# An unused 32-byte tile ahead of the weight buffers in SBUF: a conv and MLP block in fp32 on one core

## The chip, the cores and the metric

The kernel runs on one core of one Trainium2 chip. The metric is device time in microseconds (us) of one execution. Three executions of the kernel before took 1090.11, 1090.36 and 1090.12 us; the median is 1090.12 us.

## What is computed

One decoder layer on 256 tokens of width 2048, all in float32: a modulation from the condition vector c, a gated causal depthwise convolution, and an MLP of width 8192 with squared ReLU.

```python
cond = silu(c)
sh1, sc1, g1, sh2, sc2, g2 = split(cond @ mod_w + mod_b, 6)
h = rms_norm(x, norm1_g) * (1 + sc1) + sh1
a, gt = split(h @ conv_w_in + b_in, 2)          # 2048 -> 2 x 2048
u = depthwise_conv(a * sigmoid(gt), 31 taps) + dw_b
y = silu(layer_norm(u, ln_g, ln_b)) @ conv_w_out + b_out
x = x + (1 + g1) * y
h = rms_norm(x, norm2_g) * (1 + sc2) + sh2
u = square(relu(h @ mlp_w1))                    # 2048 -> 8192
x = x + (1 + g2) * (u @ mlp_w2)                 # 8192 -> 2048
```

## The kernel before, in words

**How the work is staged.** A list of jobs runs in this order: 16 jobs "in" (two 128-column blocks of conv_w_in each; the first 8 are computed together during the start), 8 jobs "out", then four quarters of the MLP with 8 jobs "up" (mlp_w1) and 8 jobs "down" (mlp_w2) each. Between them matrix-vector work for the modulation and the convolution is woven in. The order of the instructions on each engine comes from a planner that simulates a timeline, with orders put by hand where `issue_after` stands; the loads are issued by SP in the order of the list `order` (L541 to L550), each as soon as a buffer of its kind is free (`top_up`, L175).

**How a product of two float32 matrices is made.** A weight block of 1 MB comes by DMA into one of seven buffers `raw` (L181, 128 partitions of 8192 bytes). ScalarE writes the rounded part into tiles `hi` (L216), VectorE or GpSimd the rest into `lo` (L220), in halves of 4096 bytes per partition; both have the type fp32r. Activations are split in the same way into `hl` (what enters the jobs in, out and most of up) or `u2` (what enters the jobs down and, as `xa`, the first two of up). Three products hi x hi, lo x hi and hi x lo are then summed in PSUM.

In the jobs "in" and the first two "up" the weights are the stationary operand, in "out" too, in a form with 256 columns:

```python
nc.tensor.matmul(p[:, c, :], hi[:, k % HALF, :], m, ...)                       # L245, 512 columns
nc.tensor.matmul(p[:, c, T : 2 * T], lo[:, k % HALF, :], m[:, 0:T], ...)       # L246, 256 columns
nc.tensor.matmul(out_p, w, m[:, 0:T], start=begin, stop=False)                 # L241, L242, L243: 256 columns
```

In the other jobs up and down the activations are stationary, and the split weights move, 512 columns at a time (L282 to L284):

```python
hi, lo = [w[:, 4 * (k % 2) : 4 * (k % 2) + 4, :]... for w in parts[...]]
p_hi, p_lo = [m[:, n : n + P] for n in (t * P, T + t * P)]
nc.tensor.matmul(p, p_hi, hi, ...); nc.tensor.matmul(p, p_hi, lo, ...); nc.tensor.matmul(p, p_lo, hi, ...)
```

Products in plain float32 (not split) are the held first product of the jobs in (L609, weights `first`, activations `two`), the modulation rows (L336), the convolution on TensorE (L826) and column sums with the tile `ones` (L454). In the trace each of these stands as two instructions.

**Where the tiles lie.** Pools are stacked in SBUF in the order in which they are opened, and a tile starts at a multiple of 32 bytes. From the left come const, wts, acts, tmp, early and then, one after the other, start, conv or res; from the right come the pool of the four `cv` tiles with `mu` and later `pad` (L1052, 752 floats that nothing reads or writes) with `u2`. From the sizes of the tiles follow these first bytes in a partition (sizes in brackets):

| tile | first byte | past a multiple of 64 | past a multiple of 256 | past a multiple of 4096 |
|---|---|---|---|---|
| v (4624), ones (512), cz (2240) | 384, 14144, 14656 | 0 | 128, 64, 64 | 384, 1856, 2368 |
| warm (8), the last of const | 17408 | 0 | 0 | 1024 |
| raw, 7 x 8192 | 17440 | 32 | 32 | 1056 |
| hi, 6 x 4096; lo, 6 x 4096 | 74784; 99360 | 32 | 32 | 1056 |
| hl, 8 x 4096 | 123936 | 32 | 32 | 1056 |
| two, 6 x 2048 | 157728 | 32 | 32 | 2080 |
| u2, 8 x 4096 (from the right) | 193568 | 32 | 32 | 1056 |

All blocks of one kind are a multiple of 2048 bytes apart, and every operand of L241 to L246 and L282 to L284 starts a multiple of 512 bytes into its tile. The tap sums of the convolution on VectorE and ScalarE (L705, L738) read `u` from byte 4 x j of a tile on, for tap j; the matmuls L826 start 16 bytes further from one step m to the next.

Of the kernel before, what the change touches and what calls it, by code (L numbers as in the profile page):

```python
# [8 lines left out]
F32 = mybir.dt.float32  # L9
# [5 lines left out]
P = 128  # L15
# [58 lines left out]
def conv_block(ctx: ExitStack, tc: tile.TileContext, x, vec, dwq, c_row, mod_r, mod_t, mod_c, w_first, w_in, w_out, w1, w2, out):  # L74
    nc = tc.nc

    const = ctx.enter_context(tc.tile_pool(name="const", bufs=1))
# [50 lines left out]
        nc.vector.tensor_scalar(col("modb", w * KT, KT), col("modb", w * KT, KT), 1.0, None, op0=ALU.add)  # L128
    amps = {w: const.tile([P, KT], F32, name=f"amp{w}") for w in (SC1, SC2)}
    warm = const.tile([P, 2], F32, name="warm")  # L130
    other = warm[:, 1:2]

    def table(func, after):
# [1087 lines left out]
```

## Time and profile before

| what | value |
|---|---|
| median of the runs | 1090.12 us |
| span of the profiled execution, first to last instruction | 1088.4 us |
| the rest, between the span and the median | 1.7 us |
| instructions in the profile | 15427 |
| matmuls, weight loads | 6000, 6000 |

The profile was taken from one execution; its own whole time is not listed, so its span stands beside the median of the three runs. Line numbers are those of the kernel. PE is TensorE, PEld its weight loads, DVE is VectorE, ACT is ScalarE, POOL is GpSimd, SP is the engine that issues the DMAs. A matmul's duration in the trace includes the time in which it overlaps the next one, so the pace of TensorE is read from the distance between starts.

### The profile page before, as it was taken

To read this page: it belongs to the slowest core of one execution; us is meant where nothing else is said; L and a number is where in the kernel's file an instruction comes from. 1 tells how busy PE (TensorE), PEld (TensorE's weight loads), DVE (VectorE), ACT (ScalarE), POOL (GpSimd) and SP (SyncE) were. 2 spreads that over 40 slices of the span, in tenths; PEclk is the share of its full clock that TensorE was granted. 3 is DMA by queue.
4 is the path that set the end of the run, shared out by engine and by line. 5 is a ranking of instruction groups with operands and counts; after the bars stand their busy time and mean duration, and the time that the engine had idled before them with its cause. 6 is when DMAs were issued, how large, how long until landed. Compare 5 with 4: busy or idle time off the path is not lost.

```text
span 1088.4 us, 15427 instructions
## 1 busy us (share of the span) xinstructions
PE 1072.4 (99%) x6000; PEld 890.4 (82%) x6000; DVE 750.0 (69%) x1022; ACT 520.3 (48%) x707; POOL 214.6 (20%) x147
## 2 busy tenths in 40 slices
PE   6999999999999999999999999999999999999998
PEld 3888876777799988888888888888888888888887
DVE  5777799989668877778845676545565665565653
ACT  4111398776876585444444444333444333444431
POOL 0000069989498260000000000000000000000000
PEclk8999999999999999999999999999999999999999
DMA  9999997997999967999967899667888776788611
GB/s 383 420 420 421 415 418 296 375 362 272 406 409 399 363 244 237 276 288 384 390 237 227 237 283 329 202 152 291 242 237 245 222 217 212 232 251 239 212 64 39
DMA packets 142315, 314.21 MB, mean 289 GB/s; under 512 B 87585, under 2 KB 105505, under 8 KB 107297
## 3 DMA queue, kind: packets, MB, share of 16 engines
q1 hardware_dynamic: 142096, 313.10, 82.0%
q8 instruction: 47, 0.77, 0.3%
q14 instruction: 26, 0.21, 0.1%
q10 hardware_dynamic: 146, 0.13, 0.0%
HBM read 301.13 MB, written 12.07 MB: 288 GB/s over the span
## 4 chain that ended last, share of the span: by engine, by line
PE 88%; DMA 8%; DVE 2%; ACT 1%; issue 0%; ACTq 0%; SPq 0%; DVEq 0%
PE mm L283 20%; PE mm L282 20%; PE mm L284 20%; DMA raw<-mod_c 7%; PE mm L245 6%; PE mm L246 3%; PE acc L242 2%; PE acc L241 2%; PE acc L243 2%; PE mm L826 2%; PE row L336 2%; DVE raw L428 1%; PE mm L609 1%; DMA v<-vec 1%; PE mm L241 0%; PE mm L242 0%
## 5 line engine op out<-in xcount | busy, mean ns | idle before, releaser
L216 ACT ACTIVATE hi<-raw 128x1024 fp32r<-128x1024 f32 x320 | 335.3, 1058 | 358.2 <-PE mm L284 330.3
L220 DVE TENSOR_TENSOR lo<-raw,hi 128x1024 fp32r<-128x1024 f32 x259 | 314.5, 1220 | 184.0 <-ACT hi L216 182.2
L283 PE MATMUL mm<-lo,u 128*128 128x512 f32 x496 | 193.0, 389 | 0.0
L282 PE MATMUL mm<-hi,u 128*128 128x512 f32 x496 | 193.0, 389 | 0.0
L284 PE MATMUL mm<-hi,u 128*128 128x512 f32 x496 | 192.9, 389 | 0.0
L284 PE MATMUL mm<-hi,hl 128*128 128x512 f32 x480 | 186.7, 389 | 0.0
L283 PE MATMUL mm<-lo,hl 128*128 128x512 f32 x480 | 186.7, 389 | 0.0
L282 PE MATMUL mm<-hi,hl 128*128 128x512 f32 x480 | 186.7, 389 | 0.0
L220 POOL TENSOR_TENSOR lo<-raw,hi 128x1024 fp32r<-128x1024 f32 x61 | 153.5, 2546 | 31.9 <-ACT hi L216 31.9
L428 DVE SCALAR_TENSOR_TENSOR raw<-raw,cond 128x2048 f32<-128x2048 f32 x50 | 116.5, 2332 | 39.3 <-DMA raw<-mod_c 39.3
L284 PEld LDWEIGHTS mm<-hi,u 128*128 128x128 f32 x496 | 93.1, 188 | 19.3
L283 PEld LDWEIGHTS mm<-lo,u 128*128 128x128 f32 x496 | 93.1, 188 | 19.1
L282 PEld LDWEIGHTS mm<-hi,u 128*128 128x128 f32 x496 | 93.1, 188 | 19.0
L284 PEld LDWEIGHTS mm<-hi,hl 128*128 128x128 f32 x480 | 90.1, 188 | 18.7
L282 PEld LDWEIGHTS mm<-hi,hl 128*128 128x128 f32 x480 | 90.1, 188 | 18.7
L283 PEld LDWEIGHTS mm<-lo,hl 128*128 128x128 f32 x480 | 90.1, 188 | 18.7
L705 DVE SCALAR_TENSOR_TENSOR acc<-u,v,acc 128x256 f32<-128x256 f32 x230 | 91.5, 480 | 0.0
L245 PE MATMUL mm<-hl,hi 128*128 128x512 f32 x224 | 80.0, 401 | 0.0
L609 PE MATMUL mm<-two,first 128*128 128x256 f32 x240 | 57.0, 392 | 8.2 <-ACT two L667 8.0
L241 PE MATMUL acc<-hl,hi 128*128 128x256 f32 x224 | 63.4, 283 | 0.0
L242 PE MATMUL acc<-hl,hi 128*128 128x256 f32 x224 | 63.4, 283 | 0.0
L243 PE MATMUL acc<-hl,lo 128*128 128x256 f32 x224 | 63.4, 283 | 0.0
(223 smaller groups left out, 1286.7 us busy)
## 6 DMA issues: line engine op xcount, KB each, us to landing
raw<-w SPq DMA_DIRECT2D x128, 1024.0 KB, 5.5
raw<-mod_c SPq DMA_DIRECT2D x64, 1024.0 KB, 11.2
raw<-mod_r SPq DMA_DIRECT2D x28, 1024.0 KB, 9.2
raw<-w_in SPq DMA_DIRECT2D x16, 1024.0 KB, 10.9
raw<-w_out SPq DMA_DIRECT2D x16, 1024.0 KB, 7.7
first<-w_first SPq DMA_DIRECT2D x15, 1024.0 KB, 19.8
flat<-two SPq DMA_DIRECT2D x30, 256.0 KB, 2.7
two<-flat SPq DMA_DIRECT2D x120, 64.0 KB, 4.2
```

The lines of the kernel that those rows point to most:

```text
L216: state["w_hi"] = nc.scalar.activation(hi, w[:, ks, :], AF.Copy).ins
L220: end = by.tensor_tensor(lo, w[:, ks, :], hi.bitcast(F32), op=ALU.subtract)
L241: nc.tensor.matmul(out_p, w, m[:, 0:T], start=begin, stop=False)
L242: nc.tensor.matmul(out_p, w, m[:, T : 2 * T], start=False, stop=False)
L243: state["mm_end"] = nc.tensor.matmul(out_p, lo[:, k % HALF, :], m[:, 0:T], start=False, stop=end)
L245: nc.tensor.matmul(p[:, c, :], hi[:, k % HALF, :], m, start=(k == 0), stop=(k == KT - 1))
L282: nc.tensor.matmul(p, p_hi, hi, start=begin, stop=False)
L283: nc.tensor.matmul(p, p_hi, lo, start=False, stop=False)
L284: nc.tensor.matmul(p, p_lo, hi, start=False, stop=end)
L428: end = nc.vector.scalar_tensor_tensor(w, w, 1.0, cb, op0=ALU.mult, op1=ALU.mult, accum_out=acc)
L609: step = nc.tensor.matmul(held[n][:, c, :], w[:, 2 * n + c, :], h, start=k == 0 and c == 0, stop=k == KT - 1, skip_group_check=True)
L705: end = nc.vector.scalar_tensor_tensor(out, s, w, acc, op0=ALU.mult, op1=ALU.add)
```

## The change

One more tile is allocated in the pool const, after `warm` and ahead of everything in the pools that follow. Nothing writes or reads it. It has 8 floats, so 32 bytes in each partition.

```diff
     amps = {w: const.tile([P, KT], F32, name=f"amp{w}") for w in (SC1, SC2)}
     warm = const.tile([P, 2], F32, name="warm")
+    const.tile([P, 8], F32, name="shift_all")
     other = warm[:, 1:2]
```

So raw, hi, lo, hl, two and all that is stacked on them from the left begin 32 bytes further: raw at 17472, hi at 74816, hl at 123968, each 1088 bytes past a multiple of 4096 and 0 past a multiple of 64. The tiles of const itself, the cv tiles, mu and u2 stay where they are.

## Rows read from the trace of the kernel before

**Rows 1.** The page: its first line and part 1.

```profile
span 1088.4 us, 15427 instructions
PE 1072.4 (99%) x6000; PEld 890.4 (82%) x6000; DVE 750.0 (69%) x1022; ACT 520.3 (48%) x707; POOL 214.6 (20%) x147
```

**Rows 2.** Busy time by stretch: PE, PEld, DVE, ACT, POOL, clock, DMA share, GB/s.

```profile
30.00:117.00 87.00, 84.28 (x387) 72.92 (x386) 62.42 (x85) 13.57 (x26) 0.00 (x0) 1.00 1.01 420
390.00:1085.00 695.00, 694.56 (x3167) 577.76 (x3159) 436.41 (x465) 299.35 (x321) 13.96 (x6) 1.00 0.76 240
```

**Rows 3.** The chain that ended last: its shares by line, and one piece.

```profile
by line: PE mm L283 20.3%; PE mm L282 20.3%; PE mm L284 20.3%; DMA raw<-mod_c 7.3%; PE mm L245 6.3%; PE mm L246 3.1%; PE acc L241 2.5%; PE acc L242 2.5%; PE acc L243 2.5%; PE mm L826 2.0%; PE row L336 1.8%; DVE raw L428 1.4%; PE mm L609 0.9
...
54.87 19.86 DMA raw<-mod_c
```

**Rows 4.** Instructions in time, PE, job down: start us, duration us.

```profile
479.86 0.39 PE L282 MATMUL mm<-hi,u 128*128 128x512 f32 x1
...
493.46 0.39 PE L282 MATMUL mm<-hi,u 128*128 128x512 f32 x1
```

**Rows 5.** The same view, PE, job up.

```profile
575.74 0.39 PE L282 MATMUL mm<-hi,hl 128*128 128x512 f32 x1
...
589.34 0.39 PE L282 MATMUL mm<-hi,hl 128*128 128x512 f32 x1
```

**Rows 6.** The same view, PE, jobs out: 256 columns.

```profile
321.02 0.28 PE L241 MATMUL acc<-hl,hi 128*128 128x256 f32 x1
...
332.90 0.28 PE L241 MATMUL acc<-hl,hi 128*128 128x256 f32 x1
```

**Rows 7.** The chain, pieces of plain float32 matmuls: start, length, count.

```profile
127.45 1.73 PE acc L609 x8
...
162.17 3.59 PE mm L826 x64
165.76 3.43 PE row L336 x32
...
199.21 0.86 PE small L454 x4
```

**Rows 8.** Groups of instructions by line: busy us, mean ns.

```profile
L705 DVE SCALAR_TENSOR_TENSOR acc<-u,v,acc 128x256 f32<-128x256 f32 x230 | 91.5, 480 | 0.0
L738 ACT ACTIVATE cv<-u,v 128x256 f32<-128x256 f32 x22 | 9.3, 497 | 0.0
...
L1080 ACT ACTIVATE two<-x,amp 128x256 f32<-128x256 f32 x16 | 7.2, 496 | 0.0
...
L844 DVE SCALAR_TENSOR_TENSOR u<-mm,v,two 128x256 f32<-128x256 f32 x12 | 5.7, 482 | 3.3 <-ACT two L842 3.2
```

**Rows 9.** Instructions in time, PE: pairs L245 and L246, job in, then job up.

```profile
152.12 0.40 PE L245 MATMUL mm<-hl,hi 128*128 128x512 f32 x1
...
153.18 0.40 PE L245 MATMUL mm<-hl,hi 128*128 128x512 f32 x1
...
402.86 0.39 PE L245 MATMUL mm<-u,hi 128*128 128x512 f32 x1
...
408.75 0.39 PE L245 MATMUL mm<-u,hi 128*128 128x512 f32 x1
```

**Rows 10.** Matmuls that read u2 (first), then hl: ns min/median/max, first and last start.

```profile
L282 PE MATMUL mm<-hi,u x496: 389/389/396, 474.4 to 1078.0; 128*128 128x512 f32 x166
...
L282 PE MATMUL mm<-hi,hl x480: 387/389/391, 409.1 to 996.0; 128*128 128x512 f32 x160
...
L245 PE MATMUL mm<-hl,hi x224: 393/398/504, 136.5 to 250.7; 128*128 128x512 f32 x112
...
L241 PE MATMUL acc<-hl,hi x224: 283/283/283, 297.8 to 380.4; 128*128 128x256 f32 x112
```

**Rows 11.** Last use of the tiles part; the split that writes the seventh u2.

```profile
L740 POOL TENSOR_TENSOR cv<-cv,part x8: 731/741/749, 178.1 to 228.9; 128x256 f32<-128x256 f32 x8
...
361.27 0.63 ACT L228 ACTIVATE u<-two 128x512 fp32r<-128x512 f32 x1
```

## The prediction

> **What bounds the kernel now.** I read the page first. TensorE is busy for 1072.4 of 1088.4 us and VectorE, the next, for 750.0 [rows 1], so what moves an address on VectorE, ScalarE or GpSimd matters only where TensorE waits for it. Then the busy time by stretch. From 30 to 117 us the DMA share stands at 1.01 with 420 GB/s: this start is bound by loads. From 390 us to the end TensorE is busy for 694.56 of 695.00 us, while DMA is at 0.76 [rows 2]. The chain of waits says the same: L282 to L284 hold three times 20.3%, L245 and L246 9.4%, L241 to L243 7.5%, and the only transfers of weight are those into raw from mod_c, 7.3%, in pieces like the one of 19.86 us [rows 3]. So the time is about 80 us of loads and 950 us of matmuls one behind the other, and the question is whether a matmul, or a load, goes faster or slower from an address 32 bytes on.
>
> A matmul's own duration includes overlap, so I take distances between starts. In a job down, 60 steps (20 rounds of L282, L283, L284) lie between the two starts shown: (493.46 - 479.86) / 60 = 226.7 ns [rows 4]. In a job up the same 60 steps take (589.34 - 575.74) / 60 = 226.7 ns [rows 5]. With 256 columns, 99 steps take (332.90 - 321.02) / 99 = 120.0 ns [rows 6]. The difference, 106.7 ns for 256 columns, is 0.417 ns a column; 512 columns are then 213.4 ns, and 13.3 ns of every fp32r matmul do not depend on its length. Plain float32 does otherwise: eight of L609 take 1.73 us, so 216 ns for 256 columns, and 32 of L336, which run four at a time, take 3.43 us, so 429 ns for 512 [rows 7]. That is 213 ns for 256 columns, and about 3 ns fixed.
>
> **The change part by part.** *The tile itself.* It has no instruction: 0 us, and the planner has nothing new to order, so I expect the same instructions in the same order on each engine. That the tile takes room although unused follows from `pad`, which nothing uses either and which does push u2. The shift makes one new overlap between tiles from the left and from the right: the first buffer `part` ended at byte 201760, where a buffer u2 begins, and now ends 32 bytes inside it. If that adds a wait, it is for an addition that starts at 228.9 us at the latest, by a split at 361.27 us [rows 11]: 0 us.
>
> *VectorE, ScalarE, GpSimd.* The trace holds the experiment already. The tap sums L705 start at byte 4j of a tile, so at all offsets in a 64-byte block, and take 480 ns, as L844 with its fixed starts takes 482; on ScalarE the taps L738 take 497 ns and L1080, with fixed starts, 496 [rows 8]. 0 us, and what is left over would hide behind TensorE, which waits for none of them from 390 us on. GpSimd has no such pair of rows here; its 214.6 us [rows 1] lie beside the stretch that TensorE fills too. If that cover failed, a tenth of it would be 21 us, the far end of the slow side.
>
> *Plain float32 matmuls.* In L826 the moving operand starts 16 bytes further at each step m and the weights alternate between 0 and 32 past 64; its 64 instructions, four at a time, take 3.59 us, 224 ns a group with the last one's end in it. L454 reads its weights from `ones`, at 0 past 64, four in 0.86 us or 215 ns, where L609 with both operands at 32 takes 216 [rows 7]. 0 us.
>
> *Loads.* They land 32 bytes further, at 0 instead of 32 past a multiple of 64. No row here shows a full-rate load at both offsets. The stretch of 87 us moved 420 GB/s with no idle time [rows 2]; I bound this term by one 32-byte piece of the 8192 bytes of a partition, either way: 87 x 32 / 8192 = 0.34 us. I take 0 and keep -0.3 and +0.3. The Trainium skill, DMA: Bandwidth & Descriptors, section How a descriptor splits into AXI transactions, speaks against the change: a descriptor that starts off a multiple of 256 bytes also pays for the bytes below its start, so 8192 bytes from 32 past are 257 pieces of 32 bytes and from 64 past 258. By that rule the sum would be an estimated 0.3 us more, 1090.5; no run here shows it.
>
> *fp32r matmuls.* This is the term that decides, and the trace of before can't settle it: hi, lo, hl and u2 all start 1056 bytes past a multiple of 4096, so every one of these matmuls has both operands at the same offset, and the pace is the same 226.7 ns in both kinds of job [rows 4, 5]. Bounds: on the fast side the fixed 13.3 ns might shrink to the 3 ns of plain float32, 10 ns each. On the slow side the nearest row for a pace that varies is the pair L245 and L246: (153.18 - 152.12) / 3 = 353 ns in a job in, but (408.75 - 402.86) / 17 = 346.5 ns in a job up [rows 9], 3.3 ns a matmul; the far end is the fixed part paid once more, 13.3 ns. I take 0: plain float32, though slower per column, shows no trace of the start, and 60 steps in a row that come out at the same pace in two jobs look like a fixed cost of the instruction and not like a collision.
>
> The sum is 0: span 1088.4 us, and with the 1.7 us between span and median 1090.1 us. About 0.2%, 2.2 us, is what a measurement of this kernel can tell from no change.
>
> **The rivals.** *Slower: the down jobs lose the common offset.* Their weights move from 1056 to 1088 past 4096 while u2 stays, so the streams of the moving weights and of the next stationary block are no longer in step. For it: that all four kinds of tile share an offset now is what such a dependence would look like when it costs least, and u2, stacked from the other side, shares it only through the 752 floats of pad. Against it: the pace is flat, and plain float32 shows nothing. Price: 1488 matmuls (three lines of 496 [rows 10]) x 3.3 ns = 4.9 us, 1095.0; x 13.3 ns = 19.8 us, 1109.9; half way between, 8.3 ns, gives 12.4 us and 1102.5. It decides from 1.5 ns a matmul on. The up jobs would stay at 226.7 ns, since both their operands move. The Trainium skill, SBUF — State Buffer, section Who interferes with whom, gives TensorE two independent read ports, one for each stream; by that the rival would cost 0 and the time stay at 1090.1, and no run here shows the ports apart.
>
> *Faster: the fixed part was the price of 32 past 64.* Then the matmuls whose operands both move gain: 3 x 480 with 512 columns, 2 x 224 of the pair and 3 x 224 of the out jobs [rows 10], 2560, x 10 ns = 25.6 us, 1064.5; a quarter of it would be 6.4 us, 1083.7. For it: fp32r has a fixed part four times that of plain float32. Against: it is the same 13.3 ns at both lengths, as a cost of the instruction would be.
>
> *The change does nothing, since the tile gets no room.* Then 1090.1 too; `pad` speaks against it.
>
> **How the numbers follow.** No change, with both ways to get there: 0.55. Slower through the down jobs: 0.32. Faster: 0.13. The predicted time is that of the likeliest case, 1090.1 us. The range goes up to 1104, which is 9.3 ns for each of the 1488 matmuls and so holds about two thirds of the slow case, and down to 1086, which takes in the loads' bound and a third of the fast case: 0.55 + 0.21 + 0.04 = 0.80.
>
> **What would show it.** Right: 60 steps of L282 to L284 take 13.60 us in a job down and in a job up, 99 steps of L241 to L243 11.88 us, the stretch from 30 to 117 us moves 420 GB/s, and the groups of VectorE and ScalarE keep their means. The slow rival: only the steps that read u2 become longer, by more than 1.5 ns, while those with hl stay. The fast one: the steps with hl become shorter. What would make me wrong in another way is a matmul pace that changes in both kinds of job alike, or a longer split on GpSimd with TensorE waiting behind it before 390 us.

## The result and the profile after

The changed kernel takes 1099.95 us (1099.67 to 1100.13, four runs) beside 1090.21 us for the kernel before on the same chips: a ratio of 1.0089 with a 95% interval of 1.0075 to 1.0103, so 9.7 us slower. The page of the kernel after, its first line and part 1, against [rows 1]:

```profile
span 1097.8 us, 15427 instructions
PE 1081.3 (98%) x6000; PEld 888.7 (81%) x6000; DVE 750.8 (68%) x1022; ACT 521.6 (48%) x707; POOL 214.6 (20%) x147
```

The span grew by 9.4 us and TensorE's busy time by 8.9; VectorE, ScalarE and GpSimd stayed within 1.3 us, with the same counts of instructions. The 6000 matmuls stand in the same order in both traces. Every line of the new kernel behind the inserted one has a number one higher: L283 to L285 are the former L282 to L284. The same three stretches of instructions in time on TensorE, kernel after, answer to [rows 4], [rows 5] and [rows 6]: start us, duration us, then the instruction.

```profile
479.21 0.40 PE L283 MATMUL mm<-hi,u 128*128 128x512 f32 x1
...
493.21 0.40 PE L283 MATMUL mm<-hi,u 128*128 128x512 f32 x1
...
574.78 0.39 PE L283 MATMUL mm<-hi,hl 128*128 128x512 f32 x1
...
588.38 0.39 PE L283 MATMUL mm<-hi,hl 128*128 128x512 f32 x1
...
320.83 0.28 PE L242 MATMUL acc<-hl,hi 128*128 128x256 f32 x1
...
332.71 0.28 PE L242 MATMUL acc<-hl,hi 128*128 128x256 f32 x1
```

In the job down, where u2 is stationary, 60 steps now take 14.00 us, 233.3 ns each, where they took 226.7. In the job up, where hl is stationary, 60 steps take 13.60 us, 226.7 ns, and 99 steps with 256 columns 11.88 us, 120.0 ns, both as before. So the loss sits in the matmuls with 512 columns that read u2: 1488 x 6.6 ns = 9.8 us. The busy time by stretch, kernel after, shows that the loads at the start did not lose:

```profile
30.00:117.00 87.00, 83.35 (x382) 71.76 (x381) 62.28 (x86) 13.57 (x26) 0.00 (x0) 1.00 1.01 421
390.00:1085.00 695.00, 695.00 (x3102) 569.00 (x3095) 434.38 (x459) 300.57 (x321) 13.77 (x6) 1.00 0.75 240
```

DMA moves 421 GB/s from 30 to 117 us where it moved 420 [rows 2]. From 390 to 1085 us TensorE is as full as before, with 3102 matmuls in place of 3167, at a granted clock of 1.00 in both.

### The profile page after: what moved, and what is told of

It reads as the page before. It is cut to its first block, busy times and chain, and to the rows that moved or that the text cites. A ratio compares the mean times of both kernels' runs of the same rounds, so it can differ in the third digit from the quotient of the medians.

```text
span 1097.8 us, 15427 instructions
## 1 busy us (share of the span) xinstructions
PE 1081.3 (98%) x6000; PEld 888.7 (81%) x6000; DVE 750.8 (68%) x1022; ACT 521.6 (48%) x707; POOL 214.6 (20%) x147
## 4 chain that ended last, share of the span: by engine, by line
PE 87%; DMA 10%; DVE 2%; ACT 1%; issue 0%; SPq 0%; ACTq 0%
PE mm L285 20%; PE mm L284 20%; PE mm L283 20%; DMA raw<-mod_c 9%; PE mm L246 6%; PE mm L247 3%; PE acc L244 2%; PE acc L243 2%; PE acc L242 2%; PE mm L827 2%; PE row L337 2%; DVE raw L429 1%; DMA x<-x 1%; PE mm L242 0%; PE mm L243 0%; PE mm L244 0%
## 5 line engine op out<-in xcount | busy, mean ns | idle before, releaser
L284 PE MATMUL mm<-lo,u 128*128 128x512 f32 x496 | 195.9, 395 | 0.0
L285 PE MATMUL mm<-hi,u 128*128 128x512 f32 x496 | 195.9, 395 | 0.0
L283 PE MATMUL mm<-hi,u 128*128 128x512 f32 x496 | 195.9, 395 | 0.0
L285 PE MATMUL mm<-hi,hl 128*128 128x512 f32 x480 | 186.8, 389 | 0.0
L283 PE MATMUL mm<-hi,hl 128*128 128x512 f32 x480 | 186.7, 389 | 0.0
L284 PE MATMUL mm<-lo,hl 128*128 128x512 f32 x480 | 186.7, 389 | 0.0
L285 PEld LDWEIGHTS mm<-hi,u 128*128 128x128 f32 x496 | 93.0, 187 | 22.7
L284 PEld LDWEIGHTS mm<-lo,u 128*128 128x128 f32 x496 | 93.0, 187 | 22.4
L283 PEld LDWEIGHTS mm<-hi,u 128*128 128x128 f32 x496 | 93.0, 187 | 22.4
L285 PEld LDWEIGHTS mm<-hi,hl 128*128 128x128 f32 x480 | 90.1, 188 | 18.7
L283 PEld LDWEIGHTS mm<-hi,hl 128*128 128x128 f32 x480 | 90.1, 188 | 18.7
L284 PEld LDWEIGHTS mm<-lo,hl 128*128 128x128 f32 x480 | 90.1, 188 | 18.7
L706 DVE SCALAR_TENSOR_TENSOR acc<-u,v,acc 128x256 f32<-128x256 f32 x230 | 91.5, 481 | 0.0
L246 PE MATMUL mm<-hl,hi 128*128 128x512 f32 x224 | 80.1, 401 | 0.0
L610 PE MATMUL mm<-two,first 128*128 128x256 f32 x240 | 56.6, 390 | 9.0 <-ACT two L668 9.0
L243 PE MATMUL acc<-hl,hi 128*128 128x256 f32 x224 | 63.4, 283 | 0.0
```

What stands on the lines that cost most here:

```text
L243: nc.tensor.matmul(out_p, w, m[:, T : 2 * T], start=False, stop=False)
L246: nc.tensor.matmul(p[:, c, :], hi[:, k % HALF, :], m, start=(k == 0), stop=(k == KT - 1))
L283: nc.tensor.matmul(p, p_hi, hi, start=begin, stop=False)
L284: nc.tensor.matmul(p, p_hi, lo, start=False, stop=False)
L285: nc.tensor.matmul(p, p_lo, hi, start=False, stop=end)
L610: step = nc.tensor.matmul(held[n][:, c, :], w[:, 2 * n + c, :], h, start=k == 0 and c == 0, stop=k == KT - 1, skip_group_check=True)
```

## The experiments

Theory 1 was that the distance between the streams of the moving weights and the stationary activations decides. Theory 2 was that the start of the weights does by itself. "Distance" below is the first byte of the activations minus that of the weights, modulo 512, in a partition.

**u2 follows the weights.** The change is kept.

```diff
-PADDING = 752
+PADDING = 744
```

> The change is kept and u2 follows it: PADDING goes from 752 to 744, so u2 lies 32 bytes further too and every operand of the fp32r matmuls starts 1088 bytes past a multiple of 4096. Theory 1 (the distance between the moving weights and the stationary block decides): the down jobs are back at 226.7 ns a matmul, the time at 1090.1 us. Theory 2 (the start of the weights by itself decides, in down jobs only): 233.4 ns and 1099.9 us, as with the change.

Measured: 1090.43 us, ratio 1.0002 (0.9993 to 1.0012). Instructions in time, job down:

```profile
478.63 0.39 PE L283 MATMUL mm<-hi,u 128*128 128x512 f32 x1
...
492.23 0.39 PE L283 MATMUL mm<-hi,u 128*128 128x512 f32 x1
```

The 60 steps are back at 13.60 us with everything 32 bytes further than before. So at these two places, 32 and 0 past a multiple of 64, where the operands lie by themselves costs nothing.

**u2 alone moves away.** The kernel before, with no other tile moved.

```diff
-PADDING = 752
+PADDING = 760
```

> The kernel before with PADDING 760 instead of 752: u2 alone lies 32 bytes lower, the weights stay. The distance between u2 and the weights is that of the change. Theory 1 (distance): 233.4 ns a matmul in the down jobs, 226.7 in the up jobs, 1099.9 us in all. Theory 2 (start of the weights): 226.7 ns and 1090.1 us.

Measured: 1099.97 us, ratio 1.0091 (1.0074 to 1.0108). Instructions in time, job down:

```profile
478.85 0.39 PE L282 MATMUL mm<-hi,u 128*128 128x512 f32 x1
...
492.85 0.39 PE L282 MATMUL mm<-hi,u 128*128 128x512 f32 x1
```

That is 14.00 us again, and the time of the change, with the weights at their old place. Theory 2 has fallen, and the time of the change is had again to 0.1 us without it: what cost was that the weights and u2 moved apart.

**hl moves away instead.** The kernel before; u2 keeps its distance 0.

```diff
+    acts.tile([P, 8], F32, name="gap")
     hl = [None] * HALF
```

> The kernel before with the unused 32-byte tile in the pool of hl instead, ahead of hl: hl and what is stacked on it lie 32 bytes further, hi, lo and u2 stay. Theory 1 (distance): the loss moves from the down jobs to the up jobs, 1440 matmuls of 512 columns x 6.6 ns = 9.5 us, so 1099.6 us, and more if the 256-column matmuls of the jobs in and out pay as well (1344 of them with L246 and L241 to L243 and L260 to L263; at 6.6 ns up to 8 us); down jobs at 226.7 ns. Theory 2 (start of the weights): 1090.1 us, no pace changes.

Measured: 1097.71 us, ratio 1.0069 (1.0054 to 1.0084). Instructions in time: jobs out, a job down, a job up.

```profile
320.76 0.28 PE L242 MATMUL acc<-hl,hi 128*128 128x256 f32 x1
...
332.31 0.28 PE L242 MATMUL acc<-hl,hi 128*128 128x256 f32 x1
...
479.17 0.39 PE L283 MATMUL mm<-lo,u 128*128 128x512 f32 x1
...
492.77 0.39 PE L283 MATMUL mm<-lo,u 128*128 128x512 f32 x1
...
574.75 0.40 PE L283 MATMUL mm<-lo,hl 128*128 128x512 f32 x1
...
588.75 0.40 PE L283 MATMUL mm<-lo,hl 128*128 128x512 f32 x1
```

The loss has changed sides: down 13.60 us, up 14.00 us. What I had not expected was the 256-column matmuls. They were expected to pay or to stay, and became faster: 11.55 us for 99 steps, 116.7 ns in place of 120.0 [rows 6]. The sum fits: 1440 x 6.6 ns = 9.5 us up, and the first matmul of the MLP jobs with 512 moving weight columns starts at 406.96 us instead of 409.10, 2.1 us earlier; the span grew by 7.4 us.

**All distances in steps of 32 bytes.** Eight u2 tiles of their own, ua to uh, with a gap between two.

```diff
-PADDING = 752
+PADDING = 696
...
+    def new_u2(i):
+        name = "u" + "abcdefgh"[i]
+        if name not in placed and i:
+            mp.tile([P, 8], F32, name="gap" + name)
+        placed.add(name)
+        return mp.tile([P, 2, 2 * T], F32R, name=name, bufs=1)
...
```

> The kernel before with the eight u2 tiles at eight distances from the weights (modulo 512): ua at 0, then 32, 64, 96, 128, 160, 192 and uh at 224 bytes further. Theory 1 (distance): the twelve matmuls on each tile in a down job show eight paces; ua 226.7 ns, at least one other 6 ns or more longer, and if the sign of the distance doesn't matter ub is 233.4 ns. If the distance counts modulo 64 the paces repeat every second tile. Theory 2 (start of the weights): all eight at 226.7 ns and 1090.1 us.

> As the sweep before it, with ua at 256 bytes from the weights (modulo 512), then 288, 320, 352, 384, 416, 448 and uh at 480. The sweep at 0 to 224 had 226.7 ns at 0 and 230 to 233.5 ns at the seven others. If what counts is only whether the distance is 0, all eight are at 230 to 233.5 ns; if the distance counts modulo 256, ua is at 226.7 ns and the others repeat the first sweep; uh has the distance of the change (-32) and is at 233.3 ns either way.

The second has PADDING 632. They took 1097.83 and 1097.66 us, in one run each. Instructions in time of the first: the first matmul on ua, the last two on it, then the first one on some of the tiles behind it (the last line is the one that follows uh); a tile has twelve steps.

```profile
661.68 0.39 PE L282 MATMUL mm<-hi,ua 128*128 128x512 f32 x1
...
663.95 0.39 PE L283 MATMUL mm<-lo,ua 128*128 128x512 f32 x1
664.17 0.40 PE L284 MATMUL mm<-hi,ua 128*128 128x512 f32 x1
664.41 0.39 PE L282 MATMUL mm<-hi,ub 128*128 128x512 f32 x1
...
667.20 0.40 PE L282 MATMUL mm<-hi,uc 128*128 128x512 f32 x1
...
678.39 0.40 PE L282 MATMUL mm<-hi,ug 128*128 128x512 f32 x1
...
681.15 0.40 PE L282 MATMUL mm<-hi,uh 128*128 128x512 f32 x1
...
683.95 0.40 PE L282 MATMUL mm<-hi,ue 128*128 128x512 f32 x1
```

Twelve steps take 2.73 us on ua, 2.79 on ub, 2.76 on ug and 2.80 on uh. Over the whole trace the mean distance between two starts on one tile is 226.8 ns at 0 bytes and 232.9, 233.5, 233.5, 232.0, 233.4, 229.8 and 233.4 ns at 32 to 224. The second sweep, at 256 to 480 bytes, has 226.8, 232.9, 233.5, 233.5, 232.0, 233.4, 229.9 and 233.4 ns: the same row again, so the distance counts modulo 256, and a full 0 is the only one of the eight that doesn't cost. Its first and second tile:

```profile
661.51 0.39 PE L282 MATMUL mm<-hi,ua 128*128 128x512 f32 x1
...
664.24 0.39 PE L282 MATMUL mm<-hi,ub 128*128 128x512 f32 x1
```

The border between two tiles does not tell which two streams meet. The last matmul on ua has a distance of 0 from its own stationary block, but from it to the first on ub 235 ns pass in all 15 cases, 664.17 to 664.41 above; and when uh is followed by ua, the last step on uh takes 226 to 227 ns. That looks as if a step were priced by the block that is loaded during it. But from ud to ua 231 to 232 ns pass in all four cases of either sweep, although the block loaded has a distance of 0. So the mean over a row of steps follows the distance, and no rule for the single step is shown.

**Distances below 32 bytes.** The eight tiles a multiple of 512 apart, each read from 4 bytes further on.

```diff
...
+        at = [0, 1, 2, 3, 4, 5, 6, 7][i]
+        t = mp.tile([P, 4 * T + 8], F32R, name=name, bufs=1)
+        return t[:, at : at + 4 * T].rearrange("p (c n) -> p c n", c=2)
```

> The eight u2 tiles at 0, 4, 8, 12, 16, 20, 24 and 28 bytes from the weights (modulo 512). If the pace changes with blocks of 32 bytes, all eight keep 226.7 ns; with blocks of 16 bytes, ua to ud keep it and ue to uh don't; with every element, only ua keeps it. A chance that an offset inside a block is faster than 226.7 ns: one in ten.

Measured: 1098.37 us. Instructions in time, the first matmul on four of the tiles (PADDING is 232, the gaps 120 floats):

```profile
661.82 0.39 PE L282 MATMUL mm<-hi,ua 128*128 128x512 f32 x1
...
664.55 0.39 PE L282 MATMUL mm<-hi,ub 128*128 128x512 f32 x1
...
667.33 0.39 PE L282 MATMUL mm<-hi,uc 128*128 128x512 f32 x1
...
670.10 0.39 PE L282 MATMUL mm<-hi,ud 128*128 128x512 f32 x1
```

Twelve steps take 2.73 us on ua, on ub, 4 bytes on, already 2.78, and on uc 2.77. The means from 0 to 28 bytes are 227.1, 232.4, 230.6, 233.4, 233.3, 233.3, 230.8 and 235.1 ns. Nothing is seen of blocks of 16 or 32 bytes, of which two of the cases expected spoke: a single float32 is enough.

**hi and lo apart.**

```diff
-        hi, lo = [wts.tile([P, HALF, P], F32R, name=name, bufs=6) for name in ("hi", "lo")]
+        hi = wts.tile([P, HALF, P], F32R, name="hi", bufs=6)
+        if h == 0:
+            wts.tile([P, 8], F32, name="gap")
+        lo = wts.tile([P, HALF, P], F32R, name="lo", bufs=6)
```

> The kernel before with the unused 32-byte tile between hi and lo: lo and hl lie 32 bytes further, raw, hi and u2 stay. A matmul streams its moving operand while the next stationary block is loaded. Distance theory: in the up jobs (hl with lo's offset) the steps behind a stream of hi, so from L282 and L284, are longer by some 6 ns and those behind a stream of lo, from L283, keep about 226.7 ns; in the down jobs (u2 with hi's offset) it is the other way round. Averages 231.1 ns in up and 228.9 ns in down, so +6.3 and +3.3 us, less up to 2 us in the jobs in and out, where hi x hl is no longer at 0: 1097.5 to 1099.8 us. If the offsets of both streams of a whole triple count together, all steps of a triple are equally longer.

Measured: 1107.1 us in one run, 7 us over the range expected. Instructions in time, job up, then job down:

```profile
575.03 0.40 PE L282 MATMUL mm<-hi,hl 128*128 128x512 f32 x1
575.26 0.39 PE L283 MATMUL mm<-lo,hl 128*128 128x512 f32 x1
...
589.03 0.40 PE L282 MATMUL mm<-hi,hl 128*128 128x512 f32 x1
...
479.15 0.40 PE L282 MATMUL mm<-hi,u 128*128 128x512 f32 x1
...
493.15 0.40 PE L282 MATMUL mm<-hi,u 128*128 128x512 f32 x1
```

Both jobs take 14.00 us for 60 steps. The steps differ in the direction expected: behind a stream of lo 230.9 ns in up and 235.7 in down, behind a stream of hi 234.9 and 234.1 in up, 232.3 and 231.7 in down. But those at distance 0 did not stay at 226.7. Each triple comes to 700 ns, as if all three paid, but not equally, so neither of the two outcomes expected came. In this run a step at distance 0 is not fast when the streams beside it in the row have another offset. 2928 x 6.6 ns = 19.3 us, less about 2 us in the jobs in and out, is the time.

**A version that beats both.** Since 256 columns with stationary weights like a distance and 512 columns with moving weights don't, hl gets a distance in the jobs in and out alone. Its tiles are 256 bytes longer, so the distances stay modulo 256. First the two sweeps of hl that looked for a distance good for both:

```diff
+        name = "h" + "abcdefgh"[k2]
+        if name not in spaced and k2:
+            acts.tile([P, 8 if k2 else 8], F32, name="gap" + name)
+        spaced.add(name)
+        hl[k2] = acts.tile([P, 2, 2 * T], F32R, name=name, bufs=1)
```

The second has a gap of 256 bytes ahead of the first tile too.

> The eight tiles of hl at 0, 32, 64, 96, 128, 160, 192 and 224 bytes from the weights (modulo 512), u2 at 0. In the up jobs (hl stationary, weights moving) the paces are those of the first sweep: 226.7 ns for ha, 230 to 233.5 for the others. In the jobs in and out the weights are stationary and hl moves; with hl 32 bytes on, 256 columns went from 120.0 to 116.7 ns and the pair L245 and L246 from 350 to 346 ns, so hb should have these, and if any distance but 0 does it, the six others too.

> The same with 256, 288, 320, 352, 384, 416, 448 and 480 bytes. Looked for: a distance at which 256 columns take less than 120 ns and 512 columns no more than 226.7 ns; such a one, for all of hl, would beat the kernel before by up to 2 us. If 0 is the only distance with 226.7 ns, there is none.

They took 1096.1 and 1096.38 us, in one run each. In the jobs up the paces were those of u2 within 0.3 ns, again the same in both halves. With 256 columns they lay between 114.2 ns, at 448 bytes (114.4 at 192), and 119.4 ns, at 96 (119.3 at 352): no distance serves both uses. And ha at 0 had 118.3 ns, not 120.0, and hb at 32 bytes 118.7, not 116.7, so in such a mixture neighbours count. Then the three layouts:

```diff
+    def new_hl(k2, at=8):
+        t = acts.tile([P, 4 * T + 64], F32R, name="hl", bufs=HALF)
+        hl[k2] = t[:, at : at + 4 * T].rearrange("p (c n) -> p c n", c=2)
...
+        split_act(new_hl(k2, 0), h)
...
+            sqacc = x_pool.tile([P, T], F32, name="sqacc")
```

with PADDING 688, and 48, 8 or 0 for `at` in the jobs in and out.

> The kernel before with tiles of hl 256 bytes longer (sqacc moved to a later pool to make room, PADDING 688 so that u2 stays a multiple of 256 from the weights). In the jobs in and out hl is written and read 192 bytes into its tile, in the jobs up at its start. From the sweeps: up and down keep 226.7 ns; 256 columns with hl at 192 took 114.4 ns instead of 120.0, so the 768 of L241 to L243 and the 96 of L260 to L263 give 4.8 us; the 224 pairs L245 and L246 6 ns each, 1.4 us, of which about 0.6 us counted when hl lay 32 bytes on, since the jobs in also wait for other engines. Distance theory: 1084.7 to 1085.4 us. If the sweep's 114.4 ns came from the mixture of distances and a single one gives 116.7: 1087.5 us.

> The same with 32 bytes instead of 192. With hl 32 bytes on, 256 columns took 116.7 ns and the stretch up to the first MLP job was 2.1 us shorter; up and down keep 226.7 ns. Distance theory: 1088.1 us. If the new layout itself costs something, the control at 0 shows it.

> The control: the same layout with hl read at the start of its tile everywhere. All distances are multiples of 256 as in the kernel before: 226.7 and 120.0 ns, 1090.2 us.

Measured: at 192 bytes 1088.89 us (ratio 0.9984, 0.9975 to 0.9992), at 32 bytes 1088.18 us (0.9979, 0.9970 to 0.9988), the control 1090.39 us (1.0000, 0.9991 to 1.0009). Instructions in time at 32 bytes: jobs out, then a job up.

```profile
317.90 0.28 PE L241 MATMUL acc<-hl,hi 128*128 128x256 f32 x1
...
329.45 0.28 PE L241 MATMUL acc<-hl,hi 128*128 128x256 f32 x1
...
575.23 0.39 PE L282 MATMUL mm<-hi,hl 128*128 128x512 f32 x1
...
588.83 0.39 PE L282 MATMUL mm<-hi,hl 128*128 128x512 f32 x1
```

99 steps with 256 columns in 11.55 us and 60 with 512 in 13.60: both good paces in one kernel, 2.1 us faster than the kernel before and 11.8 us faster than the changed one.

Neither the 256 columns nor the stationary weights alone make the difference. In the jobs in, L245 moves 512 columns of hl past stationary weights and L246 256, in turn. At 32 bytes three of these pairs take 1.04 us, 346.7 ns each, where they took 353 [rows 9]. And the last job moves 256 weight columns at a time past u2: 45 steps take 5.40 us in the kernel before, 120.0 ns each, and 5.25 us, 116.7 ns, in the changed one, where u2 has lost distance 0. Instructions in time: pairs at 32 bytes; the last job before; the last job after.

```profile
152.23 0.39 PE L245 MATMUL mm<-hl,hi 128*128 128x512 f32 x1
...
153.27 0.39 PE L245 MATMUL mm<-hl,hi 128*128 128x512 f32 x1
...
1078.76 0.28 PE L283 MATMUL acc<-lo,u 128*128 128x256 f32 x1
...
1084.16 0.28 PE L283 MATMUL acc<-lo,u 128*128 128x256 f32 x1
...
1088.22 0.28 PE L283 MATMUL acc<-hi,u 128*128 128x256 f32 x1
...
1093.47 0.28 PE L283 MATMUL acc<-hi,u 128*128 128x256 f32 x1
```

The 114 ns of the sweep came along only in part. At 192 bytes one row in the jobs out has 39 steps in 4.42 us, 113.3 ns each, and a later one 99 steps in 11.66 us, 117.8 ns each, at the same distance:

```profile
297.86 0.28 PE L241 MATMUL acc<-hl,hi 128*128 128x256 f32 x1
...
302.28 0.28 PE L241 MATMUL acc<-hl,hi 128*128 128x256 f32 x1
...
318.33 0.28 PE L241 MATMUL acc<-hl,hi 128*128 128x256 f32 x1
...
329.99 0.28 PE L241 MATMUL acc<-hl,hi 128*128 128x256 f32 x1
```

The mean of L241 to L243 in the jobs out is 117.5 ns and the pairs stay at 353, so the layout at 192 missed both of its expected times. Two of its eleven runs took 1086.55 and 1087.35 us; whether they had more rows of the faster kind, no trace shows.

## Why the prediction was wrong

The forecast of 1090.1 us failed in one term, "fp32r matmuls", where I took 0 between 10 ns less and 13.3 ns more. It measured +6.6 ns for the matmuls that read u2 and 0 for those that read hl. The range held the time only because the slower rival was in it, and that rival is what happened: its place (the down jobs), its mechanism (the common offset lost) and its test (hl steps stay, u2 steps grow by more than 1.5 ns) were right, its middle price of 8.3 ns was too high.

The reasons for 0 were wrong in three ways. That plain float32 "shows no trace of the start" [rows 7] was true and stays true (eight L610 take 1.73 us, 64 L827 3.59 us after), but these matmuls need 216 ns for 256 columns, not 120: a stream at half the pace tells nothing of one at full pace. That 60 steps at the same pace "look like a fixed cost of the instruction" [rows 4, 5] took evenness for independence. Both rows stood at distance 0, so evenness was what a dependence on the distance would show as well. And the pace of fp32r matmuls was not flat: the same pair of instructions took 353 ns in one job and 346.5 in another [rows 9], both at distance 0, which a fixed cost does not do. I took a price from these rows and did not count them against the reason. I had named that [rows 4, 5] can't settle it, and the one hint in the kernel, that u2 shares its offset with the weights only through pad, was given too little weight.

The other steps held. No instruction was added or reordered among the matmuls. L706 takes 481 ns and L739 498, where their forerunners took 480 and 497 [rows 8]. The matmuls on hl of [rows 10] and the pairs in the jobs in [rows 9] kept their paces; the 64 pairs in the jobs up, which read u2 and so lost distance 0 too, took 0.1 us more in all. Nothing came of the overlap with part [rows 11]: the split at 361.27 us starts at 361.08 after. The 950 us of matmuls that open the prediction are more than its rows show, since all the lines of matmuls shown there have 82.5% of the chain, 898 us [rows 3]; the forecast did not use them. On the loads, the rule of the Trainium skill, DMA: Bandwidth & Descriptors, section How a descriptor splits into AXI transactions, asked for 0.3 us more as I applied it; the trace has 421 GB/s after 420 [rows 2], so nothing of it shows. That section of the Trainium skill speaks of the bytes that are fetched, and here only the place where they land moved. The rule of SBUF — State Buffer, section Who interferes with whom, also in the Trainium skill, by which the slower rival would cost nothing, does not hold here as I read it: when u2 alone was moved by 32 bytes, the pace of the 512-column steps went from 226.7 to 233.3 ns, so the times of TensorE's two reads are not independent of each other's addresses.

The faster rival is out: at 0 past 64 for all operands the pace is 226.7 ns as at 32 past 64.

What stays open is why. The sweeps show a period of 256 bytes and a price even at 4 bytes, and rows of unlike offsets or lengths follow no rule found here. Which part of the path from SBUF to TensorE does this was not found.

## What to carry to other kernels

In a long row of fp32r matmuls that each move 512 columns and load a block, keep moving and stationary operands at the same address modulo 256 bytes. Measure every other case: rows of 256 columns, and 512 and 256 in turn, were faster 32 bytes off it here. An unused tile, a new constant or another padding ahead of the buffers can change that distance by accident, so after any edit of an allocation compare the distance between starts of the same matmul in both traces, not its mean duration, before looking for another cause. An even pace over all jobs says nothing on what it depends on while nothing differs between them.

## What the runs showed that I had not expected

At the granted clock of 1.00, which is the level of 2.4 GHz, the paces are whole numbers of cycles: 226.7 ns is 544, or 512 + 32; 233.3 ns is 560, or 512 + 48; 120.0 ns is 288, or 256 + 32; 116.7 ns is 280, or 256 + 24. So moving the operands 32 bytes apart costs 16 cycles in rows of 512 moving columns and gives 8 back in rows of 256.

A distance of 0 is not enough for the fast pace. In the down job before the last, three steps with 512 columns alternate with six with 256. There the 24 steps of 512 columns take 231.8 ns on average in the kernel before, at distance 0, and 231.4 ns in the changed one: no price of the distance is left. Three of them in the kernel before, to the nanosecond 233, 236 and 228 from start to start:

```profile
1068.96 0.40 PE L282 MATMUL mm<-hi,u 128*128 128x512 f32 x1
1069.19 0.40 PE L283 MATMUL mm<-lo,u 128*128 128x512 f32 x1
1069.43 0.39 PE L284 MATMUL mm<-hi,u 128*128 128x512 f32 x1
1069.65 0.28 PE L282 MATMUL acc<-hi,u 128*128 128x256 f32 x1
```

With the two paces at 192 bytes above, this says that the distance alone does not fix the pace: the lengths of the neighbours count too, and one distance can have two paces.
